# Moving the gate sums' steps, two turns and three loads in a hybrid decoder trunk

## The chip, the cores and the metric

The kernel runs on one core of a Trainium2 chip. The metric is the device time of one execution in microseconds (us); the time before is the median of three runs, 1411.1 us (1411.07 to 1411.56). The profile is of one further execution. In its rows PE is TensorE (matrix products), PEld TensorE's loading of the stationary operand, DVE VectorE, ACT ScalarE, POOL GpSimd and SP SyncE, which issues most transfers (DMAs). A "q" behind an engine's name means its instruction queue: an issued transfer or a wait. L116 is line 116 of the kernel.

## The reference

Two decoder layers over 512 tokens of width 1024, all in float32. Layer 0 mixes tokens with a Mamba-2 SSD block, layer 1 with an HGRN2 block; the mixers are not touched by the change. After the mixer each layer does the same:

```
h = layer_norm(ALPHA * x + mix, ln_g[i,0], ln_b[i,0])
h = layer_norm(ALPHA * h + square(relu(h @ w1)) @ w2, ln_g[i,1], ln_b[i,1])
x = h + sigmoid(h @ ple_w_gate) * (p @ ple_w_proj)
```

w1 is 1024 x 4096, w2 4096 x 1024, ple_w_gate 1024 x 1024 and ple_w_proj 256 x 1024. I call the second line the MLP, `h @ ple_w_gate` the gate and `p @ ple_w_proj` the embedding product.

## The kernel before

**Split products.** Every float32 operand is split into a high part (a cast by ScalarE, L114) and a low part (a subtraction by VectorE, L116), and a product of two operands is three products of parts, L120 to L122 in `mm3`. One such instruction takes a 128 x 128 stationary and a 128 x 512 moving operand. `unit` loads 128 x 1024 weights into one of three buffers `raw` (L107, SP's queue) and splits them into a buffer of the pool `whip` (tiles whi) and one of the pool `wlop` (tiles wlo). Both pools have six buffers. A buffer comes free when its last reader is done.

**The MLP.** The hidden width is cut into four groups. A group's hidden part is eight tiles, called T: each is 8 x 3 products against one `unit`, then a ReLU by ScalarE (L528), and after each second tile a square (L530). After four tiles `half_blocks` takes the squared values apart into seven operands of Strassen-Winograd's scheme (a11, a12, a22 and the sums s1 to s4), each with a cast (L357) and a subtraction (L358), for half of the rows. A group's second product is seven block products, called Q, each again 24 products, against weights or weight sums. A Q accumulates in PSUM banks (py and pj) and VectorE adds the result to the tile `acc` (L467 to L473); each block product starts only after the banks it overwrites have been read. The order of T and Q is written out:

```
PERIODS = ("TTTTTTTT",) + 3 * ("TTQTQTQTQTQTQTQ",) + ("QQQQQQQ",)
```

In period g the T belong to group g, the Q to group g - 1. The last period has the Q of group 3 alone, and then comes the second layer norm.

**The gate's sums.** The gate too is a product in Strassen-Winograd's scheme, and its weights' sums are made ahead, during the MLP, by the generator `sums_ahead` in 20 steps of four quarters, plus a last one that ends it. A quarter is: four loads of 256 KB into one whi and one wlo buffer; two subtractions; an addition and a subtraction; a first pair of sums (cast into a tile sg by L417, stored to the DRAM tensor `pre` by ScalarE's queue, L418; the low part by L420); the first pair's low parts stored (L425) and a second pair; and with the next quarter's first step the second pair's low parts stored. Between the first load and the last store the quarter holds its two buffers. A step is taken after every Q of the periods 1 to 3, 21 in all.

**What sets the order.** TensorE's order in the MLP and the gate, and all orders on the other engines, come from a planner that works with its own costs. It picks by the order in which instructions are traced, moved forward by `tc.high_priority`; `behind(ins)` adds that an instruction is queued behind `ins` on the same engine. The sums' subtractions are queued behind `marks["acc"]`, the latest of VectorE's additions of a block product, and the stores of low parts behind `marks["act"]`, the latest ReLU.

**The gate's turns.** After the second norm `turned(c)` (in `norm_blocks`) transposes chunk c of 128 tokens of `acc` on TensorE into the banks pt and pm (L318), and ScalarE and VectorE copy and split them (L308, L309, L324, L326). There is one bank pt and one bank pm. Turn 0 is traced inside the last Q, p3, through the argument `turns`; turn 1 between the embedding products of chunks 0 and 1 (`proj(0, 0)` and `proj(1, 0)`, six products each, two steps k of three); turns 2 and 3 inside a later gate product.

**The start.** Eight loads of 384 KB (`xw`) bring a slice of x and of the first weights each, into `slots`; all are issued by SP (L163). ScalarE and VectorE split each (L170 to L176), and TensorE begins with its first six products at L698 to L702, then goes on with L120 to L122.

Of the kernel before, what the change touches and what calls it, by code (L numbers as in the profile page):

```python
# [15 lines left out]
P = 128  # L16
T = 512
# [15 lines left out]
SUMS = (60, 300, 300, 300)  # L33
# [8 lines left out]
def trunk(ctx: ExitStack, tc, a):  # L42
    nc = tc.nc
# [14 lines left out]
    uid, marks = [0], {}  # L58
# [8 lines left out]
    def f32(t):  # L67
        return t.bitcast(F32)
# [31 lines left out]
    def behind(ins):  # L100
        return nullcontext() if ins is None else tc.issue_after(ins.ins)
# [17 lines left out]
    def mm3(out, sh, sl, mh, ml, start, stop, **kw):  # L119
        nc.tensor.matmul(out, sh, mh, start=start, stop=False, **kw)  # L120
        nc.tensor.matmul(out, sh, ml, start=False, stop=False, **kw)  # L121
        marks["pe"] = nc.tensor.matmul(out, sl, mh, start=False, stop=stop, **kw)  # L122
# [36 lines left out]
    with tc.high_priority(offset=FIRST):  # L159
        slots = [acc[:, k, 0:768] for k in range(4)]  # L160
        slots += [mk(w4, [P, 2, T], "ab"[k % 2]).rearrange("p a t -> p (a t)")[:, 0:768] for k in range(4)]
        for k in range(8):
            nc.sync.dma_start(slots[k], a["xw"][k])  # L163
            if k == 3:
                dtw = mk(raws, [P, 1024], "raw")
                nc.sync.dma_start(dtw[:, :256], a["wdt"])
        for k in range(8):
            hi, lo = (v[:, k % 4, :] for v in early[k // 4])
            x, w = slots[k][:, 0:T], slots[k][:, T:768]
            nc.scalar.copy(x_s.h(k), x)  # L170
            if k == 0:
                nc.vector.tensor_copy(hi, w)
            else:
                nc.scalar.copy(hi, w)
            nc.vector.tensor_sub(lo, w, f32(hi))
            nc.vector.tensor_sub(x_s.l(k), x, f32(x_s.h(k)))  # L176
# [173 lines left out]
    def half_blocks(blk, z0, z1, p):  # L350

        ks = slice(2 * p, 2 * p + 2)
        a11, a12, a21, a22 = z0[:, :, 256:], z1[:, :, 256:], z0[:, :, :256], z1[:, :, :256]

        def put(name, f):
            hi, lo = blk[name][:, 0, ks, :], blk[name][:, 1, ks, :]
            nc.scalar.copy(hi, f)  # L357
            nc.vector.tensor_sub(lo, f, f32(hi))  # L358

        put("a11", a11)  # L360
        put("a22", a22)
        nc.vector.tensor_add(a22, a21, a22)
        put("a12", a12)
        nc.vector.tensor_sub(a21, a11, a21)
        nc.vector.tensor_sub(a11, a22, a11)
        nc.vector.tensor_sub(a12, a12, a11)
        put("s2", a11)
        put("s3", a21)
        put("s1", a22)
        put("s4", a12)  # L370
# [65 lines left out]
            us.append((hi, lo))  # L436
        return us

    def block_product(w, blk, lead, first, after=None, turns=None, sums=None):

        with behind(marks.pop(("turned", 0), None) if first else None):
            t1, t2, t3, t4 = weight_sums(w, lead)
        seen = set() if first else {(i, j) for i in range(2) for j in range(2)}
        banks = {}

        def product(x, f, name, start, i, j, turns=None):
            us = [split(v) if f in (t1, t2, t3, t4) else unit(v) for v in f]
            if start:  # L450
                banks[name] = [bank(psy, "py%d" % c) if name == "x" else bank(psj, "pj") for c in range(2)]
            t = blk[x]
            for c in range(2):
                ps = banks[name][c]
                sl = slice(c * P, (c + 1) * P)
                for k in range(4):
                    hi, lo = us[k // 2]
                    ks = slice((k % 2) * 512, (k % 2 + 1) * 512)
                    w_ = hi[:, ks], lo[:, ks]
                    mm3(ps, t[:, 0, k, sl], t[:, 1, k, sl], *w_, start and k == 0, k == 3, skip_group_check=True)  # L460
                    if turns and (c, k) == (1, 3):
                        with behind(marks["pe"]):
                            turns()
                d = acc[:, 2 - 2 * i + c, j * 512 : (j + 1) * 512]
                with tc.high_priority(offset=SOON if after else 0):
                    if after and f in (w[1][0], t1, t4, w[1][1]):
                        marks["acc"] = nc.vector.tensor_tensor_reduce(  # L467
                            d, ps, d, 1.0, 0.0, ALU.add, ALU.add, sums[:, 2 - 2 * i + c, j : j + 1]
                        )
                    elif (i, j) in seen:  # L470
                        marks["acc"] = nc.vector.tensor_add(d, ps, d)
                    else:
                        marks["acc"] = nc.vector.scalar_tensor_tensor(d, d, ALPHA, ps, ALU.mult, ALU.add)  # L473
            seen.add((i, j))

        p1 = lambda: product("a11", w[0][0], "x", True, 0, 0)
        p2 = lambda: product("a12", w[1][0], "z", True, 0, 0)
        p6 = lambda: product("s2", t2, "x", False, 1, 0)
        p7 = lambda: product("s3", t3, "y", True, 1, 1)
        p5 = lambda: product("s1", t1, "x", False, 1, 1)  # L480
        p4 = lambda: product("a22", t4, "y", False, 1, 0)
        p3 = lambda: product("s4", w[1][1], "x", False, 0, 1, turns)
        for f in (p1, p7, p6, p4, p5, p2, p3) if after else (p1, p2, p6, p7, p5, p4, p3):
            f()
            if after and f is p5:
                after(0), after(1)
            if after and f is p3:
                after(2), after(3)
            yield

    def mlp_and_gate(layer, h_s, last, turns=()):

        w1, w2 = a[f"w1_{layer}"], a[f"w2_{layer}"]
        blocks = {}
# [45 lines left out]
        for g, period in enumerate(PERIODS):  # L540
            if g < 4:
                tiles = hidden(g)
            if g > 0:
                if g == 4:
                    blk, after, turned, sums, later = norm_blocks(2 * layer + 1)
                    p_s = (mk(w4, [P, 2, T], "a", F32R), mk(w4, [P, 2, T], "b", F32R))
                    praw = mk(raws, [P, 1024], "raw")
                    nc.sync.dma_start(praw, a[f"pT_{layer}"].rearrange("p k t -> p (k t)"))
                    praw = praw.rearrange("p (k t) -> p k t", k=2)
                    nc.scalar.copy(p_s[0], praw)  # L550
                    nc.vector.tensor_sub(p_s[1], praw, f32(p_s[0]))
                w = [[[w2[8 * g - 8 + 4 * i + 2 * j + u] for u in range(2)] for j in range(2)] for i in range(2)]
                products = block_product(w, blocks.pop(g - 1), SUMS[g - 1], g == 1, *((after, lambda: turned(0), sums) if g == 4 else ()))
            for op in period:
                next(tiles if op == "T" else products)
                if 0 < g < 4 and op == "Q":
                    next(ahead, None)
                if g == 4:
                    for _ in ahead:
                        pass  # L560
# [14 lines left out]

        pus, pps, held = {}, {}, {}

        def proj(c, h, parts=1):
            if h not in pus:
                pus[h] = unit(a[f"wp_{layer}"][h])  # L580
            pu = pus[h]
            pps[c, h] = []
            n = 512 // parts
            for i in range(parts):
                pp = bank(psj, "pj")[:, :n]
                for k in range(2):
                    ks = slice(k * 512 + i * n, k * 512 + (i + 1) * n)
                    mm3(pp, p_s[0][:, k, c * P : (c + 1) * P], p_s[1][:, k, c * P : (c + 1) * P], pu[0][:, ks], pu[1][:, ks], k == 0, k == 1)
                pps[c, h].append(pp)

        def product(x, f, c, ps, start, hook=()):
            cs = slice(c * P, (c + 1) * P)
            for k in range(4):
                hi, lo = f[k // 2]
                ks = slice((k % 2) * 512, (k % 2 + 1) * 512)
                mm3(ps, blk[x][:, 0, k, cs], blk[x][:, 1, k, cs], hi[:, ks], lo[:, ks], start and k == 0, k == 3, skip_group_check=True)
                for at in hook:
                    if (c, k) == at[:2]:
                        with behind(marks["pe"]):
                            turned(at[2])  # L600
# [15 lines left out]
                late.append(lambda: turn(h, c))  # L616

        two = lambda p, tag: [bank(p, tag % c if "%" in tag else tag) for c in range(2)]
        proj(0, 0)
        with behind(marks["pe"]):  # L620
            turned(1)
        proj(1, 0)
        xb = two(psy, "py%d")
        f = [unit(v) for v in wb[0][0]]
        for c in range(2):
# [864 lines left out]
```

## Time and profile before

| | |
|---|---|
| median of three runs | 1411.1 us |
| the profiled execution | 1411.54 us |
| its span, first to last instruction | 1409.8 us |
| TensorE busy | 1400.4 us (99%) |
| VectorE busy | 1076.0 us (76%) |
| ScalarE busy | 777.6 us (55%) |
| DMA | 214.70 MB, 152 GB/s over the span |

A row of a timeline reads: start, duration (both us), engine, line, operation, tile written <- tiles read, shapes, count, and in brackets how long the engine had been idle and what ended that. Ends of TensorE's products are modelled and overlap, so its pace is read from starts. A wait for several things is put down to the one that came last. A row of the chain reads: start, duration, what. A row of windows has, for each stretch, the busy time of each engine, TensorE's granted clock, the busy share of the DMA engines and their GB/s. A row of waits has who waited for what, the total, how often, and the longest.

### The profile page before, as it was taken

To read this page: it belongs to the slowest core of one execution; us is meant where nothing else is said; L and a number is where in the kernel's file an instruction comes from. 1 tells how busy PE (TensorE), PEld (TensorE's weight loads), DVE (VectorE), ACT (ScalarE), POOL (GpSimd) and SP (SyncE) were. 2 spreads that over 40 slices of the span, in tenths; PEclk is the share of its full clock that TensorE was granted. 3 is DMA by queue.
4 is the path that set the end of the run, shared out by engine and by line. 5 is a ranking of instruction groups with operands and counts; after the bars stand their busy time and mean duration, and the time that the engine had idled before them with its cause. 6 is when DMAs were issued, how large, how long until landed. Compare 5 with 4: busy or idle time off the path is not lost.

```text
span 1409.8 us, 20492 instructions
## 1 busy us (share of the span) xinstructions
PE 1400.4 (99%) x7973; PEld 1168.9 (83%) x7973; DVE 1076.0 (76%) x1777; ACT 777.6 (55%) x1164; POOL 1.8 (0%) x11
## 2 busy tenths in 40 slices
PE   9999999999999999999999999999999999999998
PEld 7888888888988888887888888888898888888787
DVE  7997877696866878787985774776785877868986
ACT  7886666573554555545564446465454554544563
POOL 0000000000000000000000000000000000000000
PEclk9999999999999999999999999999999999999999
DMA  8423333323354646655473321222163566565364
GB/s 295 157 98 135 103 108 120 105 90 105 129 185 143 228 161 204 211 176 177 139 280 122 104 92 62 89 92 75 61 239 122 171 209 214 175 215 194 108 246 154
DMA packets 66819, 214.70 MB, mean 152 GB/s; under 512 B 7713, under 2 KB 8353, under 8 KB 66593
## 3 DMA queue, kind: packets, MB, share of 16 engines
q1 hardware_dynamic: 57504, 196.59, 41.6%
q10 hardware_dynamic: 9216, 16.78, 3.3%
q8 instruction: 63, 1.03, 0.3%
q14 instruction: 36, 0.29, 0.1%
HBM read 194.41 MB, written 18.94 MB: 151 GB/s over the span
## 4 chain that ended last, share of the span: by engine, by line
PE 96%; DMA 1%; DVE 1%; ACT 1%; issue 1%; SPq 0%; DVEq 0%; ACTq 0%
PE pj L120 25%; PE pj L122 24%; PE pj L121 24%; PE py L120 5%; PE py L122 5%; PE py L121 5%; PE py L881 1%; PE py L1147 1%; PE py L883 1%; DVE wlo L116 1%; PE pt L864 0%; DMA raw<-in_whvg 0%; DMA acc<-in_xw 0%; ACT whi L114 0%; DMA pre<-whi 0%
## 5 line engine op out<-in xcount | busy, mean ns | idle before, releaser
L116 DVE TENSOR_TENSOR wlo<-raw,whi 128x1024 fp32r<-128x1024 f32 x222 | 269.4, 1221 | 171.6 <-ACT whi L114 170.4
L114 ACT CAST whi<-raw 128x1024 fp32r<-128x1024 f32 x222 | 232.8, 1051 | 302.3 <-PE pj L121 157.5
L120 PE MATMUL pj<-b,whi 128*128 128x512 f32 (+1 forms) x1000 | 379.6, 380 | 0.0
L121 PE MATMUL pj<-b,whi 128*128 128x512 f32 (+1 forms) x1000 | 377.3, 377 | 0.0
L122 PE MATMUL pj<-b,wlo 128*128 128x512 f32 (+1 forms) x1000 | 377.3, 377 | 0.0
L122 PEld LDWEIGHTS pj<-b,wlo 128*128 128x128 f32 x1000 | 188.2, 188 | 34.8
L121 PEld LDWEIGHTS pj<-b,whi 128*128 128x128 f32 x1000 | 188.2, 188 | 34.2
L120 PEld LDWEIGHTS pj<-b,whi 128*128 128x128 f32 x1000 | 188.0, 188 | 34.1
L122 PE MATMUL pj<-whi,b 128*128 128x512 f32 x530 | 206.1, 389 | 0.0
L120 PE MATMUL pj<-whi,b 128*128 128x512 f32 x496 | 196.1, 396 | 0.0
L121 PE MATMUL pj<-wlo,b 128*128 128x512 f32 x496 | 193.2, 390 | 0.0
L114 ACT CAST whi<-r 128x1024 fp32r<-128x1024 f32 x64 | 67.2, 1053 | 96.6 <-PE pj L121 79.9
L122 PEld LDWEIGHTS pj<-whi,b 128*128 128x128 f32 x530 | 99.5, 188 | 20.7 <-DVE b L1342 0.2
L120 PEld LDWEIGHTS pj<-whi,b 128*128 128x128 f32 x496 | 93.2, 188 | 20.3 <-ACT k L1076 0.5
L121 PEld LDWEIGHTS pj<-wlo,b 128*128 128x128 f32 x496 | 93.2, 188 | 18.5
L120 PE MATMUL py<-whi,b 128*128 128x512 f32 x256 | 100.7, 393 | 3.1 <-ACT b L357 3.1
L122 PE MATMUL py<-whi,b 128*128 128x512 f32 x256 | 99.8, 390 | 0.0
L121 PE MATMUL py<-wlo,b 128*128 128x512 f32 x256 | 99.7, 389 | 0.0
L116 DVE TENSOR_TENSOR wlo<-r,whi 128x1024 fp32r<-128x1024 f32 x64 | 77.8, 1220 | 27.8 <-ACT whi L114 24.0
L120 PEld LDWEIGHTS py<-whi,b 128*128 128x128 f32 x256 | 48.0, 188 | 15.0 <-ACT b L357 3.9
L122 PEld LDWEIGHTS py<-whi,b 128*128 128x128 f32 x256 | 48.1, 188 | 10.1
L121 PEld LDWEIGHTS py<-wlo,b 128*128 128x128 f32 x256 | 48.1, 188 | 9.7
(374 smaller groups left out, 1934.1 us busy)
## 6 DMA issues: line engine op xcount, KB each, us to landing
raw<-in_w SPq DMA_DIRECT2D x112, 512.0 KB, 3.4
r<-in_w SPq DMA_DIRECT2D x64, 512.0 KB, 4.0
raw<-in_wssd SPq DMA_DIRECT2D x38, 512.0 KB, 3.6
a<-csd SPq DMA_DIRECT2D x16, 512.0 KB, 3.6
raw<-in_wso SPq DMA_DIRECT2D x16, 512.0 KB, 3.7
pre<-sg ACTq DMA_DIRECT2D x32, 256.0 KB, 3.0
whi<-pre SPq DMA_DIRECT2D x16, 512.0 KB, 5.3
wlo<-pre SPq DMA_DIRECT2D x16, 512.0 KB, 6.6
```

Of the source, the lines that this page charges most:

```text
L114: nc.scalar.copy(hi[:, :n], f)
L116: nc.vector.tensor_sub(lo[:, :n], f, f32(hi[:, :n]))
L120: nc.tensor.matmul(out, sh, mh, start=start, stop=False, **kw)
L121: nc.tensor.matmul(out, sh, ml, start=False, stop=False, **kw)
L122: marks["pe"] = nc.tensor.matmul(out, sl, mh, start=False, stop=stop, **kw)
L881: nc.tensor.matmul(yd[64 * r : 64 * r + 64, sl], xdt[:, c, r, :], m[:, r, sl], start=True, stop=c == 0)
L883: nc.tensor.matmul(yd[64 * r : 64 * r + 64, sl], pv[:, c - 1, r, :], ecs[:, r, (c - 1) * P : c * P], start=False, stop=True,)
L1147: nc.tensor.matmul(ps[r][32 * b : 32 * b + 32, base + n * c : base + n * c + n], kk[r][:, ts], moving(r, 4 * c + b), start=True, stop=True,)
```

## The change

Three things change. The first three of the eight first loads are cut in two by partitions; SP issues the half of partitions 0 to 63, ScalarE's queue the other. The sums' steps are taken after each T of the periods 1 to 3 instead of after each Q; as the first T of period 1 come before any block product, `half_blocks` now sets `marks["acc"]` too, at each of its subtractions, so that a step's subtractions are queued behind the later of the two. Turn 0 is traced inside `proj(0, 0)` after its first three products, turn 1 inside `proj(1, 0)` after its first three; the argument `turns` goes.

```
         for k in range(8):
-            nc.sync.dma_start(slots[k], a["xw"][k])
+            if k < 3:
+                nc.sync.dma_start(slots[k][0:64], a["xw"][k][0:64])
+                nc.scalar.dma_start(slots[k][64:P], a["xw"][k][64:P])
+            else:
+                nc.sync.dma_start(slots[k], a["xw"][k])
...
         def put(name, f):
             hi, lo = blk[name][:, 0, ks, :], blk[name][:, 1, ks, :]
             nc.scalar.copy(hi, f)
-            nc.vector.tensor_sub(lo, f, f32(hi))
+            marks["acc"] = nc.vector.tensor_sub(lo, f, f32(hi))
...
                     mm3(ps, t[:, 0, k, sl], t[:, 1, k, sl], *w_, start and k == 0, k == 3, skip_group_check=True)
-                    if turns and (c, k) == (1, 3):
-                        with behind(marks["pe"]):
-                            turns()
...
-        p3 = lambda: product("s4", w[1][1], "x", False, 0, 1, turns)
+        p3 = lambda: product("s4", w[1][1], "x", False, 0, 1)
...
             for op in period:
                 next(tiles if op == "T" else products)
-                if 0 < g < 4 and op == "Q":
+                if 0 < g < 4 and op == "T":
                     next(ahead, None)
...
-        def proj(c, h, parts=1):
+        def proj(c, h, parts=1, turn=None):
...
                     mm3(pp, p_s[0][:, k, c * P : (c + 1) * P], p_s[1][:, k, c * P : (c + 1) * P], pu[0][:, ks], pu[1][:, ks], k == 0, k == 1)
+                    if turn == c and k == 0:
+                        with behind(marks["pe"]):
+                            turned(c)
...
-        proj(0, 0)
-        with behind(marks["pe"]):
-            turned(1)
-        proj(1, 0)
+        proj(0, 0, turn=0)
+        proj(1, 0, turn=1)
```

More of the change, by code (lines that the diff above doesn't have):

```diff
@@ L437, in ready, with block_product @@
         return us
-    def block_product(w, blk, lead, first, after=None, turns=None, sums=None):
+    def block_product(w, blk, lead, first, after=None, sums=None):
         with behind(marks.pop(("turned", 0), None) if first else None):
@@ L446, in block_product, with product @@
         banks = {}
-        def product(x, f, name, start, i, j, turns=None):
+        def product(x, f, name, start, i, j):
             us = [split(v) if f in (t1, t2, t3, t4) else unit(v) for v in f]
@@ L552, in mlp_and_gate @@
                 w = [[[w2[8 * g - 8 + 4 * i + 2 * j + u] for u in range(2)] for j in range(2)] for i in range(2)]
-                products = block_product(w, blocks.pop(g - 1), SUMS[g - 1], g == 1, *((after, lambda: turned(0), sums) if g == 4 else ()))
+                products = block_product(w, blocks.pop(g - 1), SUMS[g - 1], g == 1, *((after, sums) if g == 4 else ()))
             for op in period:
                 next(tiles if op == "T" else products)
-                if 0 < g < 4 and op == "Q":
+                if 0 < g < 4 and op == "T":
                     next(ahead, None)
```

## The prediction

> **What bounds the kernel now.** I read the page first, then the waits of TensorE's weight loader over the whole span, then the timelines around the four largest of them.
>
> ```profile
> span 1409.8 us, 20492 instructions
> PE 1400.4 (99%) x7973; PEld 1168.9 (83%) x7973; DVE 1076.0 (76%) x1777; ACT 777.6 (55%) x1164; POOL 1.8 (0%) x11
> ...
> PEld py L120 <- ACT b L357: 3.9, 2, 2.2
> PEld py L120 <- ACT whi L174: 1.6, 2, 0.9
> PEld py L120 <- DVE acc L471: 1.5, 4, 0.4
> PEld pt L318 <- ACT b L324: 1.1, 2, 0.7
> ...
> 651.71 0.39 PE L120 MATMUL pj<-b,whi 128*128 128x512 f32 x1
> ...
> 654.20 0.39 PE L122 MATMUL pj<-b,wlo 128*128 128x512 f32 x1
> ```
>
> TensorE is the bound: where nothing is missing it starts a 128x512 product every 0.227 us (the last two rows are the first and the last of twelve: 2.49 us for eleven steps), and a faster VectorE or ScalarE is worth nothing except where TensorE waits. The second part lists waits (total, times, longest). The kernel can gain only from such rows, and the change touches four: the two of 3.9 us are the hand-over from the last weight group of an MLP to the one before the norm (one per layer), L174 is the start, L318 the gate turns. The row L471 is a tail of the hand-over. I price each by TensorE's own starts: the gap between two starts less the usual 0.23.
>
> The hand-over of layer 0, and after the dots that of layer 1:
>
> ```profile
> 655.98 1.06 ACT L530 ACTIVATE b<-b 128x1024 f32<-128x1024 f32 x1
> 658.96 2.00 ACT L114 CAST whi<-r 128x1024 fp32r<-128x1024 f32 x2 [1.92 <-DMA pre<-whi]
> 660.04 2.36 DVE L116 TENSOR_TENSOR wlo<-r,whi 128x1024 fp32r<-128x1024 f32 x2 [2.00 <-PE py L122]
> 662.32 0.69 DVE L358 TENSOR_TENSOR blk<-b,blk 128x512 fp32r<-128x512 f32 x1
> 662.92 1.22 DVE L116 TENSOR_TENSOR wlo<-r,whi 128x1024 fp32r<-128x1024 f32 x1
> 664.06 1.29 DVE L358 TENSOR_TENSOR b<-b,b 128x512 fp32r<-128x512 f32 x2
> 665.08 0.39 PE L122 MATMUL pj<-whi,blk 128*128 128x512 f32 x1
> 665.26 0.68 DVE L362 TENSOR_TENSOR b<-a,b 128x512 f32<-128x512 f32 x1
> 665.87 0.68 DVE L471 TENSOR_TENSOR acc<-py,acc 128x512 f32<-128x512 f32 x1
> 665.98 0.62 ACT L357 CAST b<-b 128x512 fp32r<-128x512 f32 x1 [2.51 <-DVE b L362]
> 666.70 0.47 PE L120 MATMUL py<-whi,b 128*128 128x512 f32 x1 [1.23 <-ACT b L357]
> ...
> 1307.44 4.07 DMA pre<-whi
> ...
> 1311.53 2.00 ACT L114 CAST whi<-r 128x1024 fp32r<-128x1024 f32 x2 [2.54 <-DMA pre<-whi]
> 1317.04 0.39 PE L122 MATMUL pj<-whi,blk 128*128 128x512 f32 x1
> 1319.27 0.47 PE L120 MATMUL py<-whi,b 128*128 128x512 f32 x1 [1.84 <-ACT b L357]
> ```
>
> Read it backwards. TensorE stands from 665.08 to 666.70, which is 1.62 less 0.23 = **1.4 us** lost, and from 1317.04 to 1319.27, **2.0 us**. It is released as L471 (the addition that empties the bank py of the product before; it ends 666.55) and the cast L357 (ends 666.60) are done; the view names the cast, which came last by 0.05 us, but the product writes that bank, so I hold L471 for as good a releaser. Both stand at the end of a queue of VectorE work without a hole from 660.04 on: 5.8 us until L471 starts. That queue could not start because ScalarE's cast L114 waited 1.92 us (2.54 in layer 1), though ScalarE was free at 655.98 + 1.06 = 657.04. What it waited for is a store: the last gate-weight sum, written out from a buffer of the pool whi, which the cast was to reuse. A store takes 4.07 us from issue to landing here. So a side job, the sums, sits at the one place where the work has no slack.
>
> **Part 1, the sums' steps move from behind a Q to behind a T.** Nothing is added or removed: the same 21 steps per layer, with their loads on SP's queue, stores on ScalarE's queue, subtractions on VectorE and casts on ScalarE. There are 7 Q but 8 T in each of the three mixed periods, so the last step moves from the last Q of the third to its fifth T. That is seven operations of 24 products earlier, 7 x 24 x 0.23 = 38 us. The stores of the last pair then land long before 657, and the buffer is not held. The first half of the gain is certain if the planned order holds: the wait of 1.92 and 2.54 us on a store goes away.
>
> How much of it reaches TensorE? Bounds first. At best all of it: -1.4 - 2.0 = -3.4 us, and with the small L471 waits (1.5 less four times 0.23 = 0.6) -4.0. At worst the two casts find no buffer earlier either, as these are given back by TensorE: if the first had to wait for the end of the Q at work, which lies 24 products before the stop (665.08 - 24 x 0.227 + 0.39 = 660.0), nothing is won. I take a value between them by counting buffers. With the sums' buffer back there are six, so the first cast gets one from the T before, whose products are all done by 655.98, as its result is being squared there. The second needs the first weight tile of the Q at work, which 18 of its 24 products read: that Q and the 24 products after it end with the start at 665.08, so it began at 665.08 - 47 x 0.227 = 654.4, and its eighteenth product ends at 654.4 + 17 x 0.227 + 0.39 = 658.7. The second cast ran at 658.96 + 0.95 = 659.9, so the queue behind it comes 1.2 us earlier. In layer 1, counted the same way from 1317.04, it moves from 1312.5 to 1310.7, 1.8 us. Both are less than what TensorE lost, so all of it counts: **-3.0 us**.
>
> What is late next: the steps that moved. Each step's stores can now hold a buffer elsewhere. What such holds cost today:
>
> ```profile
> ACT whi L114 <- DMA pre<-whi: 11.9, 7, 2.8
> ACT whi L114 <- DMA pre<-sg: 6.5, 3, 2.2
> ACT whi L114 <- DMA pre<-wlo: 3.5, 1, 3.5
> ```
>
> Eleven casts wait for a store, 21.9 us in all, and nine of them leave no wait of TensorE: the rows that TensorE's list has for these stretches are the ones above. The cover is the next T or Q, 24 x 0.227 = 5.4 us of products whose weights are cast already. I price the moved steps at nothing on that ground; without cover the price is the third rival's. The new mark in half_blocks puts the subtractions of a step after the fourth and eighth T behind the last of that helper's subtractions, two to four of 0.69 us on VectorE; the loads stand in SP's queue among the same weight loads as now, and the stores of low parts are tied to the ReLU of the T just placed instead of the one before, an instruction that ScalarE reaches earlier than now, as the T itself is earlier. Nobody waits for a sum before the gate.
>
> **Part 2, the turns.** Turn 0 moves from the end of the last MLP product to the middle of the first embedding product, turn 1 from between the two embedding products to the middle of the second: three products later by the code for turn 0. The same eight transposes and copies each.
>
> ```profile
> 701.92 1.05 ACT L114 CAST whi<-raw 128x1024 fp32r<-128x1024 f32 x1 [0.58 <-DMA raw<-in_wg]
> 702.85 0.40 PE L122 MATMUL pj<-whi,b 128*128 128x512 f32 x1
> 703.51 0.66 PE L318 MATMUL pt<-cst,acc 128*128 128x128 f32 x4 [0.26 <-ACT b L324]
> ...
> 1355.34 0.39 PE L122 MATMUL pj<-whi,b 128*128 128x512 f32 x1
> 1355.71 0.55 PE L318 MATMUL pt<-cst,acc 128*128 128x128 f32 x3
> ```
>
> Turn 1 waits for the one bank pt, which the copy L324 of turn 0 empties; TensorE loses 703.51 - 702.85 - 0.23 = 0.43 us and 0.14 in layer 1. Before turn 1 stand nine products of the embedding; in the new order six by the code (or nine again, if the planner puts turn 1 where it expects the bank empty). With nine, turn 0's copies are 0.7 us later, the wait stays hidden behind the same products and the loss stays or goes: 0 to -0.57. With six the wait grows by at most 3 x 0.23 a layer, +1.4 in all. The cast of L114 holds the copy back in either case. I take **-0.2**.
>
> **Part 3, the first loads.**
>
> ```profile
> 0.73 1.28 ACT L170 ACT_TABLE_LOAD   x1 [0.73 <-PEq L1476]
> 0.74 1.81 SPq L163 DMA_DIRECT2D acc<-in_xw  x4
> 3.60 0.62 ACT L170 CAST b<-acc 128x512 fp32r<-128x512 f32 x1 [1.59 <-DMA acc<-in_xw]
> 4.40 0.71 PE L698 MATMUL py<-b,whi 128*128 128x512 f32 x2
> 9.77 0.39 PE L120 MATMUL py<-b,whi 128*128 128x512 f32 x1
> ...
> 1.64 6.04 DMA acc<-in_xw
> ...
> 1.75:2.75 1.00, 1.00 (x7) 1.00 (x7) 0.00 (x0) 0.26 (x1) 0.00 (x0) 1.00 0.98 332
> 5.75:7.75 2.00, 1.50 (x6) 0.78 (x5) 1.03 (x2) 0.78 (x3) 0.00 (x0) 1.00 0.87 292
> 9.75:12.75 3.00, 3.00 (x14) 2.44 (x13) 2.71 (x7) 2.61 (x6) 0.00 (x0) 1.00 1.04 409
> ```
>
> From 4.40 to 9.77 TensorE starts 15 products, which need 15 x 0.23 = 3.4 us: 2.0 us are lost to loads two and three; the third takes 6.04 us. The last two numbers of the window rows are the DMA engines' busy share and GB/s: they are busy 0.87 to 0.98 from the first microsecond and move 292 to 332, later 409. SP issues a load each 0.45 us (1.81 for four), the engines need 1 to 2 us for one. So issuing is not what is slow, and a second queue gives the same engines the same bytes: value near nothing. Best case -2.0 (all waits gone). Worst case: the first cast needs both halves, and ScalarE's come only after its table load, 1.28 us late: +1.3. If its three issues go first, the table load ends at 0.73 + 3 x 0.45 + 1.28 = 3.4, still before 3.60. The first casts of ScalarE and VectorE then wait for two landings instead of one, and only the rest of the start is queued behind them. SP's own three issues stay three, so its later loads are issued no later. I take **-0.3**, nearest to the rows of busy engines.
>
> [...]
>
> **Sum.** -3.0 - 0.2 - 0.3 = -3.5 us. The profiled execution took 1411.54 us (span 1409.8 and 1.7 around it), 0.4 above the median of 1411.1; by it 1408.0, by the median **1407.6 us**. I tell no change from up to 0.2%, that is 2.8 us: 1408.3 to 1413.9 is "same".
>
> **The rivals.** (1) *The wait changes its owner.* The casts at the hand-over wait for buffers of the Q at work, and VectorE's queue of 5.8 us stays as long, so TensorE still waits. For it: the second cast needs such a buffer, and that queue is longer than the 5.4 us of a Q. Against: the first cast waited for nothing but the store. It leaves 0 to -1.2 us of part 1: about 1410.5 without the other parts. (2) *Everything pays.* Loads two and three arrive in time (-2.0), the hand-over waits nowhere (-3.4), turn 1 neither (-0.57): 1411.1 - 6.0 = 1405.1. For it: in both layers the wait on the store (1.92, 2.54) is longer than what TensorE lost (1.4, 2.0); against: the busy DMA engines. (3) *Slower: a moved store meets the wrong cast.* At the fourth T of the third period the step's store, up to 3.5 us of waiting by the row above, holds a cast in front of that period's half_blocks; VectorE's queue of 5.8 us follows it, 9.3 us against a cover of 5.4: 3.9 us a layer, 7.8 together, less the 3.5 won, 1415.4. It decides as soon as wait and queue together exceed the cover there. Against it: nine such waits are covered today. (4) *The change does nothing of what it says,* because the planner orders by its own costs and keeps the sums late: 1411, counted with the first.
>
> **How the numbers follow.** Forecast 0.45 (own range 1406.2 to 1409.0), rival 1 with 4 0.28, rival 2 0.18, rival 3 0.09. Faster than 1408.3: three quarters of the forecast, and rival 2: 0.34 + 0.18 = 0.52, taken as 0.53. Same: the rest of the forecast and rival 1: 0.39. Slower: 0.08. The range for eight in ten goes from beyond rival 2 (all bounds of the parts below: -4.0 - 0.6 - 2.0 = -6.6, 1404.5, and half a microsecond for the unseen) to the whole of rival 1 and a bad start: 1404.0 to 1411.9; rival 3 is left out.
>
> **What would show it.** Part 1 is right if no cast L114 near 657 and 1309 waits for a store and TensorE's gaps there fall from 1.62 and 2.23 to under 0.8; wrong if the gap stays with another releaser. Part 2: the gap before turn 1. Part 3: landing of the third load (7.7 now) and the start of product 15 (9.77). Two facts would make the number wrong: a new wait of TensorE over 1 us anywhere in the mixed periods, or product 15 starting before 8.5.

## The result and the profile after

The changed kernel takes **1416.39 us** (median of 6 runs, 1416.12 to 1418.05) against 1411.78 for the kernel before in its 6 runs (1411.07 to 1412.1): ratio **1.0034**, 95% interval 1.0023 to 1.0044. It is slower; the forecast was 1407.6. The profiled execution took 1416.5 us, with a span of 1414.5 against 1409.8, so there are 4.7 us to be found.

The waits of TensorE's weight loader, changed kernel (total, times, longest):

```profile
PEld py L120 <- DVE acc L472: 8.1, 5, 3.6
...
PEld py L700 <- ACT b L174: 1.4, 1, 1.4
...
PEld pm L322 <- ACT b L330: 0.4, 2, 0.2
```

The rows of 3.9 us (two waits for a cast) and 1.5 us (four waits for L471) of before have become one row of 8.1: 5.4 us grew by **2.7**. A new wait stands at the start (L700). The row of 1.1 us for the turns has become one of 0.4.

The hand-over of layer 0 in the changed kernel's timeline; L361 and L362 are the casts and subtractions of half_blocks, L424 and L429 the low subtractions and low stores of the sums, L472 the addition that empties a bank:

```profile
661.15 0.39 PE L122 MATMUL py<-whi,blk 128*128 128x512 f32 x1
...
661.91 0.62 ACT L361 CAST blk<-b 128x512 fp32r<-128x512 f32 x1
...
663.05 0.69 DVE L362 TENSOR_TENSOR blk<-b,blk 128x512 fp32r<-128x512 f32 x1
663.65 0.68 DVE L424 TENSOR_TENSOR whi<-whi,sg 128x512 fp32r<-128x512 f32 x1
...
664.37 0.33 ACTq L429 DMA_DIRECT2D pre<-whi  x1
...
668.81 1.05 ACT L114 CAST whi<-r 128x1024 fp32r<-128x1024 f32 x1 [1.47 <-DMA pre<-whi]
...
669.50 0.39 PE L122 MATMUL pj<-whi,blk 128*128 128x512 f32 x1
...
672.24 0.69 DVE L472 TENSOR_TENSOR acc<-py,acc 128x512 f32<-128x512 f32 x1
...
672.98 0.50 PE L120 MATMUL py<-whi,b 128*128 128x512 f32 x1 [3.08 <-DVE acc L472]
```

The store that was to go early goes late. The tile blk of a period's s4 is shared with the period before, whose last Q reads it until 661.15 + 0.39. Only then can s4 be cast (661.91) and its low part be taken (663.05). That subtraction is the mark behind which the sums' last two subtractions are issued, so these run from 663.65 on, though they read nothing of half_blocks. In the kernel before they ran 9.5 us earlier, behind an addition of a block product:

```profile
654.14 0.69 DVE L420 TENSOR_TENSOR whi<-whi,sg 128x512 fp32r<-128x512 f32 x1
...
654.86 0.33 ACTq L425 DMA_DIRECT2D pre<-whi  x1
```

The cast that takes over the sums' buffer starts at 668.81 instead of 658.96, and TensorE stands 3.08 us instead of 1.23. In layer 1 it stands 3.18 us, and there something else follows. Windows behind the stand of layer 0 (first row) and of layer 1 (TensorE's granted clock is the third number from the end):

```profile
673.00:676.00 3.00, 3.00 (x13) 2.31 (x14) 3.00 (x4) 0.21 (x1) 0.00 (x0) 1.00 0.00 0
...
1326.40:1327.00 0.60, 0.60 (x4) 0.50 (x3) 0.60 (x2) 0.00 (x0) 0.00 (x0) 0.85 0.00 0
1327.00:1328.00 1.00, 1.00 (x4) 0.72 (x3) 1.00 (x2) 0.00 (x0) 0.00 (x0) 0.50 0.00 0
...
1330.00:1331.00 1.00, 1.00 (x5) 0.79 (x4) 1.00 (x3) 0.00 (x0) 0.00 (x0) 0.88 0.00 0
```

Behind the first stand the clock stays at 1.00. Behind the second it is halved (the microseconds left out read 0.50 too) for 0.6 x 0.30 + 3.0 + 0.24 = 3.4 us. Products start 0.43 us apart there (1327.09, 1327.52, 1327.95) instead of 0.23, and 3.4 us at half pace cost **1.7 us** of products.

The start of the changed kernel, ScalarE and TensorE:

```profile
0.73 2.12 ACTq L165 DMA_DIRECT2D acc<-in_xw  x3
4.03 1.28 ACT L174 ACT_TABLE_LOAD   x1 [4.03 <-DMA acc<-in_xw]
5.32 0.62 ACT L174 CAST b<-acc 128x512 fp32r<-128x512 f32 x1
...
5.99 1.22 PE L700 MATMUL py<-b,whi 128*128 128x512 f32 x2 [1.16 <-ACT b L174]
```

The table load, at 0.73 before, waits for a landing and starts at 4.03; the first cast comes at 5.32 instead of 3.60. As a yardstick for the start I take the first transposition of bm, behind which all the kernels do the same work; in before and after it stands at:

```profile
41.15 0.49 PE L781 MATMUL pt<-cst,bm 128*128 128x128 f32 x3
```

```profile
42.42 0.49 PE L783 MATMUL pt<-cst,bm 128*128 128x128 f32 x3
```

So the start costs **1.3 us** in this execution. About half a microsecond of it seems to go with the execution and not with the loads: here the products start 0.42 to 0.5 us apart until 9.14. In two other profiled executions with the same halved loads (the experiments with the old mark and with part 3 alone) the first four take 1.0 us instead of 1.9, and the yardstick stands at 41.91 and 41.78, 0.8 and 0.6 us behind before. Whole loads too have it anywhere from 40.38 to 41.24, in six profiles. The account is 1.3 (start) + 2.7 (hand-overs) + 1.7 (clock) = 5.7, less some 0.7 for the turns: 5.0, against 4.7 of span.

### The profile page after: what moved, and what is told of

Same layout as the page of the kernel before. It is cut to its first block, busy times and chain, and to the rows that moved or that the text cites. A ratio compares the mean times of both kernels' runs of the same rounds, so it can differ in the third digit from the quotient of the medians.

```text
span 1414.5 us, 20512 instructions
## 1 busy us (share of the span) xinstructions
PE 1402.0 (99%) x7973; PEld 1171.6 (83%) x7973; DVE 1076.4 (76%) x1777; ACT 775.2 (55%) x1164; POOL 1.8 (0%) x11
## 4 chain that ended last, share of the span: by engine, by line
PE 97%; DVE 1%; DMA 1%; ACT 0%; issue 0%; DVEq 0%; ACTq 0%
PE pj L120 25%; PE pj L122 24%; PE pj L121 24%; PE py L120 5%; PE py L121 5%; PE py L122 5%; PE py L883 1%; PE py L1149 1%; PE py L885 1%; DMA pre<-whi 1%; PE pt L866 0%; PE pt L230 0%; DVE b L362 0%; PE pt L826 0%; PE pt L1318 0%; PE py L1257 0%
```

## The experiments

Eleven kernels ran in three groups, each group beside runs of the kernel before on the same chip (medians 1413.05, 1412.6 and 1413.1 there), so ratios are compared.

### The mark as it was

```diff
-            marks["acc"] = nc.vector.tensor_sub(lo, f, f32(hi))
+            marks.setdefault("acc", nc.vector.tensor_sub(lo, f, f32(hi)))
```

> The changed kernel with one thing undone: the helper half_blocks no longer moves the mark behind which the sums' subtractions are issued (it only sets it where none is set yet, before the first Q); the steps stay behind a T, the turns and the halved loads stay. Theory A (the mark): in the changed kernel the last pair's subtractions stand behind the subtraction for s4 at 663.05, whose tile the Q at work holds, so their stores land at 668.8 and 669.4 and the cast at the hand-over waits 1.5 us for them; without the mark the stores land before 657 in layer 0 and before 1309 in layer 1, no cast there waits for a store, TensorE's two waits of 3.5 and 3.6 us shrink to under 1 us each, and the time falls from 1416.4 by 4 to 7 us, to 1409.5 to 1412.5. Rival B (the move itself): a step behind T loads its buffers at a place where they are missed, whatever the mark; the waits of 3.5 us stay and the time stays within 1 us of 1416.4.

Measured: 1406.62 us, ratio **0.9962** (0.9948 to 0.9976). Which instruction the subtractions follow turns the loss into a gain. Its timeline:

```profile
5.41 0.62 ACT L174 CAST b<-acc 128x512 fp32r<-128x512 f32 x1
...
622.79 0.33 ACTq L429 DMA_DIRECT2D pre<-whi  x1
...
659.45 1.06 ACT L114 CAST whi<-r 128x1024 fp32r<-128x1024 f32 x1 [0.49 <-PE py L122]
...
668.90 0.63 PE L120 MATMUL py<-whi,b 128*128 128x512 f32 x2
```

The last stores go out from 622.79 on, 41.6 us earlier than in the changed kernel, no cast of the hand-over waits for them, and TensorE runs through it (the first row, of the start, is used further below). Rival B is out: the waits on a store are gone, as theory A has it. The time is below the 1409.5 to 1412.5 that theory A gave (9.8 us below the changed kernel by medians, though from different chips).

### One part at a time

Part 1 alone, part 3 alone and part 2 alone, on the kernel before. The edit of the first; the others are the change's own lines for the loads and for the turns:

```diff
-                if 0 < g < 4 and op == "Q":
+                if 0 < g < 4 and op == "T":
...
-            nc.vector.tensor_sub(lo, f, f32(hi))
+            marks["acc"] = nc.vector.tensor_sub(lo, f, f32(hi))
```

> The kernel before with part 1 alone (the sums' steps behind a T, with the mark in half_blocks). Theory A, by the gaps between TensorE's starts: this part alone costs 1.7 us in layer 0 and 2.6 us in layer 1, so 1411.8 + 4.3 = 1416.1. Rival C: the loss comes from the parts together (start and turns shift the stretch), and this part alone costs under 2 us: below 1413.8.

> The kernel before with part 3 alone (three first loads halved, the upper halves from ScalarE's queue). Theory A: ScalarE's table load runs behind the wait for the first half, at 4.0 instead of 0.7, so the first cast is at 5.3 instead of 3.6 and the dt products at 15.9 instead of 14.65; nothing later makes it good: 1411.8 + 1.3 = 1413.1. Rival C: a later stretch has slack for it, 1411.8 within 0.4.

> The kernel before with part 2 alone (the two turns inside the embedding products). Theory A, by the gaps between TensorE's starts: -0.9 us in layer 0 and -0.15 in layer 1, 1411.8 - 1.0 = 1410.8. Rival C: the turns' gain in the changed kernel is a by-product of the later hand-over, and alone this part is worth 0 within 0.3: 1411.8.

Part 1 alone: 1415.95 us, ratio **1.0024** (1.0013 to 1.0035), as theory A has it (1416.1). It carries the loss of the hand-overs without help from the others; its span is 1414.1. Its waits, and the windows behind its stands in layer 0 and (last row) layer 1:

```profile
PEld py L120 <- DVE acc L471: 8.2, 5, 3.6
```

```profile
672.00:676.00 4.00, 4.00 (x12) 3.15 (x13) 4.00 (x5) 0.17 (x1) 0.00 (x0) 0.67 0.00 0
676.00:680.00 4.00, 4.00 (x17) 3.29 (x16) 2.34 (x5) 1.73 (x2) 0.00 (x0) 0.90 0.37 131
...
1326.00:1330.00 4.00, 3.35 (x14) 2.61 (x15) 4.00 (x6) 0.89 (x1) 0.00 (x0) 1.00 0.02 4
```

The same row as in the changed kernel, 8.2 for 8.1, and the half clock again, this time in layer 0 and not in layer 1: 8.2 - 5.4 + 4 x 0.33 + 4 x 0.10 = 4.5, against 1414.1 - 1409.8 = 4.3.

Part 3 alone: 1413.59, ratio 1.0007 (0.9998 to 1.0016). Part 2 alone: 1411.76, ratio 0.9992 (0.9984 to 1.0001). By these intervals neither is told from no change, nor theory A from rival C: both keep the old hand-over, and their runs spread over 4 to 5 us, as do those of the kernel before beside them (1410.96 to 1415.79). This hides a microsecond. The clock has a part in the spread: of those 23 runs of the kernel before, the ones with a mean granted clock of 0.997 took 1414.15 us or more, the two with 1.000 took 1411.26 and 1412.29. In the profiled execution of part 2 alone TensorE stood 2.78 us at the hand-over of layer 1 (1.84 before), and the clock halved there too:

```profile
1319.13 0.77 PE L120 MATMUL py<-whi,b 128*128 128x512 f32 x1 [2.78 <-ACT b L357]
```

```profile
1318.00:1319.00 1.00, 0.00 (x0) 0.00 (x0) 1.00 (x3) 0.58 (x2) 0.00 (x0) 0.70 0.20 82
...
1325.00:1326.00 1.00, 1.00 (x6) 0.77 (x5) 0.00 (x0) 0.00 (x0) 0.00 (x0) 0.89 0.00 0
```

(between the two rows 0.50 in each microsecond.) So the smaller parts are better compared on a kernel whose hand-over is clean; the runs of the two kernels that follow spread over 1.0 and 1.6 us.

### With a clean hand-over: whole loads, and without the turns

```diff
-            if k < 3:
-                nc.sync.dma_start(slots[k][0:64], a["xw"][k][0:64])
-                nc.scalar.dma_start(slots[k][64:P], a["xw"][k][64:P])
-            else:
-                nc.sync.dma_start(slots[k], a["xw"][k])
+            nc.sync.dma_start(slots[k], a["xw"][k])
```

> The kernel of the run with the old mark, with the first three loads whole and from SP's queue again: parts 1 (without its mark) and 2 alone. Theory A: the start is that of the kernel before (first cast at 3.6, dt products at 14.65) and nothing later makes up for the 1.3 us, so 1406.6 - 1.2 = 1405.4, span 1403.6. Rival C: later stretches have slack for a late start: 1406.6 within 0.3.

> The kernel before with the sums' steps behind a T and nothing else (the mark as before, the turns at their old places, whole loads). Theory A: the turns are worth 0.9 us in layer 0 and 0.15 in layer 1 wherever the hand-over stands, so this is 1.0 us above the run with whole loads: about 1406.4. Rival C: 0 within 0.3, 1405.4. Against the kernel before it prices the move of the sums without its mark: 1406.4 is 5.4 below 1411.8, more than the 3.4 us that TensorE stood at the two hand-overs in the profile of before.

With whole loads: **1404.79 us**, ratio **0.9943** (0.9931 to 0.9956), the best of all and better than both kernels. Without the turns as well: 1405.95, ratio 0.9952 (0.9939 to 0.9964). That last kernel differs from before in the word "T" for "Q" and in an initial mark, and saves 5.8 us of span (1409.8 to 1404.0). Its yardstick stands at

```profile
40.83 0.49 PE L781 MATMUL pt<-cst,bm 128*128 128x128 f32 x3
```

which is 0.3 earlier than before. The rest can be read product by product, the n-th start of TensorE's 7973 against the n-th of before: this kernel is 0.36 us ahead in front of the hand-over of layer 0 and 2.36 behind it, 3.19 in front of that of layer 1 and 5.73 behind it. So **4.5 us** (2.0 and 2.5) are the hand-overs'; 0.8 more come in the gate of layer 0, whose lines the edit does not touch. By the medians the gain is larger (6.7 us), which fits the lower clock in some runs of the kernel before (0.997 to 0.999 in nine of the eleven beside these). Neither kernel has a wait for L471 or for the cast L357 left; their rows for the turns are

```profile
PEld pm L318 <- ACT b L326: 0.4, 2, 0.2
```

```profile
PEld pt L318 <- ACT b L324: 0.7, 2, 0.4
```

The first is with the turns inside the products, the second without. By the profiles the turns are worth 0.3 us, and the start of the second was 0.4 later (40.83 against the 40.38 below), though both have the same loads. The medians differ by 1.2 us, the median spans by 0.5 (1403.0 and 1403.5). So theory A's 1.0 fits the medians and rival C's 0 within 0.3 the profiles; these five runs of each don't decide between them.

### What in the halved loads costs

Against the run with the old mark (1406.62), whole loads save 1.8 us by medians. ScalarE's first rows with whole loads, and the yardstick:

```profile
0.74 1.28 ACT L170 ACT_TABLE_LOAD   x1 [0.74 <-PEq L1474]
3.84 0.62 ACT L170 CAST b<-acc 128x512 fp32r<-128x512 f32 x1 [1.82 <-DMA acc<-in_xw]
...
40.38 0.49 PE L779 MATMUL pt<-cst,bm 128*128 128x128 f32 x3
```

Four kernels take the halves apart. A tiny copy first, so that the table load has nothing to wait for:

```diff
+        warm = mk(sm, [P, 1], "lnsd")
+        nc.scalar.copy(warm, zero[:, 0:1])
```

> The run with the old mark (halved loads) with one tiny copy of ScalarE added, of a zeroed column into a column that nobody reads, so that its table load waits for no landing. Theory T (the table load behind the wait is the loss): the table load ends before 3.5, the first cast starts when the later half has landed, at 4.8 instead of 5.3, and with the halves' late landing as the rest of the loss the time is 0.4 to 0.6 us below 1406.6. Rival D (the table load is all of it): the first cast is back at 3.6 to 3.9 and the time at 1405.4. Rival E (the halves' landings alone): first cast still at 5.3, 1406.6.

Measured: 1408.06, ratio 0.9966 (0.9953 to 0.9978), **above** 1406.62 and so outside all three. The copy changed the order of ScalarE's casts, and load three's, whose halves had landed by 8.37, waited until 8.98 for load four; this run decides nothing. The same with the casts tied to the order of the loads:

```diff
-            nc.scalar.copy(x_s.h(k), x)
+            with behind(marks.get("x")):
+                marks["x"] = nc.scalar.copy(x_s.h(k), x)
...
-                nc.scalar.copy(hi, w)
+                with behind(marks["x"]):
+                    marks["x"] = nc.scalar.copy(hi, w)
```

> As the run with the tiny copy first, and ScalarE's casts of the start tied to the order of the loads, so that the cast of load four no longer stands ahead of that of load three (in the run before, the third cast waited until 8.98 for the fourth load, though both halves of the third had landed by 8.37). Theory T (two faults: the table load behind the wait, and later landings of halves): first cast at 4.7, third at 8.0 to 8.4, time between 1404.8 (whole loads) and 1406.6 (halves with the late table load): 1405.5 to 1406.3. Rival D (the table load is all): 1404.8 within 0.3. Rival E (it is none of it): 1406.6 or above.

Measured: 1406.76, ratio 0.9959 (0.9946 to 0.9973). Its start:

```profile
1.35 1.28 ACT L154 ACT_TABLE_LOAD   x1 [1.35 <-PEq L1482]
...
4.84 0.62 ACT L177 CAST b<-acc 128x512 fp32r<-128x512 f32 x1 [2.01 <-DMA acc<-in_xw]
...
5.52 1.22 PE L704 MATMUL py<-b,whi 128*128 128x512 f32 x2 [0.69 <-ACT b L177]
...
8.24 0.63 PE L120 MATMUL py<-b,whi 128*128 128x512 f32 x1
8.67 0.63 PE L121 MATMUL py<-b,whi 128*128 128x512 f32 x1
...
42.67 0.49 PE L787 MATMUL pt<-cst,bm 128*128 128x128 f32 x3
```

The table load is out of the way, and the first cast, now released by the later half, is at 4.84 instead of 5.41, yet nothing is won: rival E gives the time, with another reason than it named. The later half lands at 4.8, a microsecond behind a whole load, TensorE stands 0.69 us, and from then until 10.37 products follow each other by 0.43 us (8.24 to 8.67) instead of 0.227. In part 3 alone, with the same halves, they follow by 0.23 to 0.42 (7.95 to 8.37, 9.04 to 9.27). In the profiled execution of this kernel the half microsecond won at the cast went there, and more: the yardstick is at 42.67 against 41.91 with the old mark. Whether the other runs also start at half pace isn't shown, as they have no profile; their medians are equal within 0.2 us. So the late table load alone isn't the loss.

All halves from SP's queue:

> The halved loads all from SP's queue (six issues of 64 partitions), with the old mark. ScalarE's table load is as early as in the kernel before (0.7 to 2.0). Theory T: what is left of the loss is that each half takes as long to issue as a whole load (0.57 us in the changed kernel, against 0.45 for a whole one), so both halves of the first load have landed by 4.2, the third load lands later than in the changed kernel (8.2), at about 9, and the time is 0 to +1.0 us on 1405.4. Rival D: halving is free when ScalarE issues nothing: 1405.4 and third load by 7.8.

Measured: 1408.63, ratio 0.9969 (0.9958 to 0.998), 3.8 us above whole loads; both theories had less, and both had the table load as early as in the kernel before.

```profile
4.88 1.28 ACT L174 ACT_TABLE_LOAD   x1 [4.88 <-DMA acc<-in_xw]
```

ScalarE issues nothing here, and its table load waits all the same, for the second half, which lands at 4.81. So it isn't the issuing that holds it. Last, halves by columns on both queues, where each cast needs one landing:

```diff
+                nc.sync.dma_start(slots[k][:, 0:T], a["xw"][k][:, 0:T])
+                nc.scalar.dma_start(slots[k][:, T:768], a["xw"][k][:, T:768])
```

> The first three loads halved by columns instead of partitions: the 512 columns of x from SP's queue, the 256 of the weight from ScalarE's; all else as in the run with whole loads. The same six issues on the same two queues, but each first cast waits for one landing. Theory T (a cast that waits for two landings hands one wait to the table load ahead of it): the table load runs right after ScalarE's three issues, at 2.2 to 2.9, and the first cast at 3.7 to 4.3; time 1404.8 to 1405.8. Rival F (ScalarE's issues themselves hold the table load): the table load again at about 4, first cast at 5.3, 1406.6.

Measured: 1405.44, ratio 0.995 (0.9938 to 0.9963), as theory T has it; rival F is out.

```profile
0.73 1.38 ACTq L165 DMA_DIRECT2D acc<-in_xw  x3
2.14 1.28 ACT L174 ACT_TABLE_LOAD   x1 [2.14 <-issue]
3.73 0.62 ACT L174 CAST b<-acc 128x512 fp32r<-128x512 f32 x1 [0.31 <-DMA acc<-in_xw]
...
40.76 0.49 PE L783 MATMUL pt<-cst,bm 128*128 128x128 f32 x3
```

Same queues, same six issues: the table load waits for no landing and the first cast is at 3.73. Where the cast needed two landings, the table load ahead of it waited for one of them (it ran at 4.03 in the changed kernel, at 4.88 with all halves from SP); where it needed one, it didn't (0.74 with whole loads, 2.14 here). Why the later of two halves of 64 partitions lands at 4.8 (the earlier at 3.9 to 4.1) when the whole load lands at 3.6 to 3.8 and column halves at 3.7 and 3.9 is not settled.

### A mark that is not held

```diff
+            if name == "a11":
+                marks["acc"] = low
```

> The run with whole loads, with the mark in half_blocks again but set by the subtraction for a11 alone, the first of the helper, whose tile no Q at work holds. Theory A (it is the held tile of s4 that keeps the sums' last subtractions back): the stores of the last pair land before 657 and the time is 1404.8 within 0.5. Rival G (any mark in half_blocks moves the subtractions of the step behind work that comes late): a wait on a store at the hand-over again, 1407 or more.

Measured: 1405.43, ratio 0.9951 (0.9939 to 0.9964): 0.1 us beyond theory A's 1404.8 within 0.5, and far from rival G's 1407. The last store of a pair goes out at

```profile
621.51 0.33 ACTq L427 DMA_DIRECT2D pre<-whi  x1
```

A mark in half_blocks does no harm by itself; the one on s4, whose tile a Q still reads, does. That it is the tile that keeps s4 back rests on the rows: its cast follows the Q's last product at 661.15 in the changed kernel, and at 660.87 follows the one at 659.64 in the kernel before.

## Why the prediction was wrong

**Part 1, -3.0 forecast, +4.3 measured alone by the spans of the profiles (+2.9 by medians).** The step that failed is the price of the new mark: "two to four of 0.69 us on VectorE", set at nothing because VectorE's time was counted and not the moment from which the marked instruction can run. With it fell "The stores of the last pair then land long before 657": they were issued at 664.37. The prediction saw the mark and asked how long the instruction takes; it did not ask who reads the tile that it writes. The mechanism behind the gain was right: with the mark left alone, no cast of the hand-over waits for a store. There the gain at the hand-overs is 4.5 us, not 3.0, and the step that was too small is the limit by the second cast. That cast came where the prediction put it. In the kernel with nothing but the sums moved it starts at

```profile
658.35 1.05 ACT L114 CAST whi<-r 128x1024 fp32r<-128x1024 f32 x1 [0.49 <-PE py L122]
```

and, with the 0.36 us that this kernel was ahead added, at 658.71, against 658.7 forecast (in layer 1 at 1307.47, with 3.19 added 1310.66, against 1310.7). But TensorE's gain isn't the cast's. The planner's order of products changed too: where TensorE started 12 products into bank pj at the hand-over (662.59 to 665.08 before) and then needed py, it now starts 24 and runs through into py. It won 2.0 and 2.5 us instead of 1.2 and 1.8, more even than the bound of -4.0. That the new order of products gave the rest is likely; no run separates it.

**Rivals.** The slower one (1415.4) came closest in time, by luck, as its way was another: it put a waiting cast in front of half_blocks at the fourth T, while the wait stayed at the hand-over and grew there. Rival 1, a new owner of the wait, had the casts wait "for buffers of the Q at work". A Q at work was the cause, but through a tile of VectorE's output and the order of issue. Rival 3 took its price from stores that wait in the kernel before; there the sums' subtractions follow an addition, and not a write into a tile that a Q still reads.

**Part 2, -0.2 forecast.** By the profiles with a clean hand-over -0.3, within the bounds of 0 to -0.57 (the medians give more, and don't settle it). The gap before turn 1 went, and 0.4 us of short waits at the second bank came.

**Part 3, -0.3 forecast, +0.6 to +1.3 measured by the yardstick.** Two steps failed. "the table load ends at 0.73 + 3 x 0.45 + 1.28 = 3.4, still before 3.60" assumed that it runs as soon as ScalarE's issues are through; it ended at 5.31. And "The first casts of ScalarE and VectorE then wait for two landings instead of one" was written down without a price; the later half landed a microsecond after a whole load. The bound of +1.3 was the right size by luck: it had the later half issued behind the table load, while the load itself ran late, and part of the 1.3 is half pace. A second issuing queue gained nothing with the column halves either (1405.44 against 1404.79 with whole loads, intervals overlapping).

**Not in the prediction at all** is the half clock behind a long stand, 1.7 of the 4.7 us. Of the facts named as what would make the number wrong, "a new wait of TensorE over 1 us anywhere in the mixed periods" came nearest: not new, but grown, at their end.

## What to carry to other kernels

An order "issue this behind that" costs what *that* waits for, not what it takes (here 9.5 us, with an instruction of 0.69): before such a mark is moved, look up who still reads the tile that the marked instruction writes. Where a cast needs two landings, look at what stands ahead of it on its engine, a table load above all (4.03 and 4.88 here, against 0.73 before), and price the later landing (4.8 against 3.8). Compare small parts of a change only on a kernel from which the large, varying wait is gone.

## What the runs showed of the hardware

**A stand of TensorE can cost twice.** Of five stands of 2.78 to 3.19 us, in three profiled executions, three were followed by a halved clock and two were not; shorter ones at the hand-overs were not (the longest, in part 3 alone, took 2.43 us). The half clock lasted 3.4 us twice and, with the stand of 2.78, 0.6 + 6.0 + 0.2 = 6.8, the first 0.7 of them inside the stand. The length of a stand doesn't tell the two kinds apart: in part 1 alone 3.19 us in layer 0 was followed by a halved clock and 3.18 in layer 1 was not, and the shortest of the five, 2.78, had the longest half clock. What does tell them apart isn't shown by these runs.

**The clock row of a start is no measurement.** In the start of the run with the table load first and ordered, products follow each other by 0.43 us, while the clock's row reads 1.00:

```profile
8.00:9.00 1.00, 1.00 (x4) 0.81 (x3) 0.49 (x3) 0.66 (x2) 0.00 (x0) 1.00 1.08 395
...
10.37 0.39 PE L122 MATMUL py<-b,wlo 128*128 128x512 f32 x1
10.60 0.40 PE L120 MATMUL py<-b,whi 128*128 128x512 f32 x1
```

From 10.37 on they follow by 0.23. In the changed kernel, too, they follow by 0.42 to 0.5 us up to 9.14 while the row reads 1.00, and the first clock record of its trace stands at 9.27 (4.32 in before): for time without a record the view prints 1.00. The spacing of the products is the safer reading in a start.
